# Side transfers on another queue, and decays and scans at other ticks, in a hybrid attention and state-space block

## The chip, the core and the metric

The kernel runs on one core of one Trainium2 chip. The metric is the device time of one execution in microseconds, the median of three runs. A profile of one execution shows each engine's instructions: TensorE (PE, its weight loads PEld), VectorE (DVE), ScalarE (ACT), GpSimd (POOL) and SyncE (SP), which only issues transfers here.

## The reference

One layer and a final norm on x of 256 rows and 2048 columns, in float32:

```
hn = rms_norm(x)
q, k, v, z_a, z_s, xbc, dt, g_a, g_s = split(hn @ w_in)
o_a = sum over three dilated windows of softmax-weighted attention(q, k, v) * silu(z_a)
xs, B, C = split(silu(causal_conv(xbc)))
y = chunked state-space scan of xs * dt with decays exp(cumsum(dt * a)), chunks of 128 rows
y = rms_norm((y + d_skip * xs) * silu(z_s))
merged = sigmoid(g_a) * (o_a @ w_attn) + sigmoid(g_s) * (y @ w_ssm)
out = rms_norm(x + merged @ w_out)
```

Sixteen attention heads of 128 columns; eight groups of the state-space part with eight heads of 64 columns each.

## The kernel before

**Weights and splits.** All weights lie in one array `wall`, cut into units of 128 x 1024 floats (512 KB) in the order in which they are used (`weight_plan`, `FIRST[tag]` is a tag's first unit). `unit(n)` takes a unit from a ring of five slots (`ring`, tag "w", loaded by SP's queue), rounds it to a high part `h` on ScalarE and leaves the rest as a low part `l` on VectorE; h and l have four buffers each. Every product is made of three parts, high by high, high by low and low by high.

**Gemms.** `gemm_a` makes 128 output columns from two units: for each of 16 blocks a matmul of 512 moving columns with h (L329) and one of 256 with l (L332). `gemm_b` makes a gate. `gemm_pair` makes 1024 output columns for v, the attention gate, and the three output projections; it goes over quads (two blocks of rows and two of columns) in an order given by hand (`V_ORDERS` and the like). A quad named in `S_QUADS` takes seven products instead of eight. It needs sums of weight blocks and sums of blocks of the left matrix.

**Side work.** `sum_jobs` makes the sums of weight blocks ahead of time, 37 jobs: `get` loads two pieces, `add` (three units later) subtracts them on VectorE and `spill` writes the sum to DRAM; 18 jobs lie in the groups' loop (place `sums_at`), 19 in the attention (place `th_a`). `keep_left` makes the sums of a left matrix (x, y or o) with `turn_x` and spills them; `fetch_left` reads them back before they are used. All this is hung on units with `behind_unit(n, f)`: f is called once unit n has been converted and gets a piece of h, `behind`. Each transfer is held back by a one-column copy on GpSimd from `behind` into the tile that the transfer then writes (`fetch`, L638, and L247, L251, L432, L903); the transfers themselves are issued by SP, those of `fin` and `fw` by ScalarE.

**Ticks.** Each gemm (each two units of `gemm_b`, each quad of `gemm_pair`) begins with `tick()`; `after(n, f)` calls f n ticks later. In the loop over eight groups (per group one B and one C gemm, four gemms each of xs and zs) the work of a group hangs on the tick of its last xs gemm: `turn` 3 later (L801), four `decays` 2, 3, 4 and 9 later (each loads `acb` by SP and issues six activations, L782 and L786), `scan` 11 later (L820), and then `gather`, which writes yT. Before two of the groups gate gemms add to the lags. After the last group one gate gemm follows, and `tick(final=True)` calls all that is still due.

**Order.** A planner with a simulated timeline orders each engine's instructions within their dependencies, with priorities given in the code; what stands here is the program that it made. `tc.issue_after(ins)` adds an edge: every instruction made in its block on the engine of `ins` stays behind `ins` in that engine's queue.

**Pools.** The left factors of x for v and the attention gate are quads 2, 4, 5, 6 (`SX_X`) and 3 (`SX_V`). Quad 2's has a pool of its own (`xk`), which opens before the pool of the output projection of the state-space part; the others' (`xl`, `vx`) open after it, where that pool was.

Of the kernel before, what the change touches and what calls it, by code (L numbers as in the profile page):

```python
# [15 lines left out]
P = 128  # L16
# [4 lines left out]
GROUPS = 8  # L21
# [14 lines left out]
N_ACT_X = 1  # L36
DT_LAG, CB_LAG, TURN_LAG, GT_LAG, Y_LAG, S_LAG, M_LAG = 2, 5, 3, 2, 11, 2, 2
Y_AFTER = 0, 0
GS_BEFORE = {0: (0, 1), 4: (2,)}
A_ORDERS = {0: (0, 1, 2, 4, 3, 6, 5, 7), 2: (0, 2, 1, 4, 3, 5, 6, 7)}  # L40
V_ORDERS = {0: (0, 2, 4, 1, 3, 5, 6, 7), 2: (0, 2, 1, 4, 3, 5, 6, 7)}
G_ORDERS = {c: (0, 2, 1, 4, 3, 5, 6, 7) for c in (0, 2)}
# [154 lines left out]
def hybrid_block(ctx: ExitStack, tc: tile.TileContext, wall, xt, x, pk_d, cst_d, fw_d, out):  # L197
# [32 lines left out]
    ssm_pool = []  # L230

    def behind_unit(n, f):
        on_unit.setdefault(n, []).append(f)
# [4 lines left out]
    def spill(kept, key, name, src, shape):  # L238
        kept[key] = dram.tile([P, *shape], F32, name=name, tag=name)
        nc.sync.dma_start(kept[key], src)  # L240

    def sum_jobs(jobs, units, places):

        def get(tag, q, t, b11, behind):
            n = FIRST[tag] + 2 * q
            for dst, src in ((t, wall[n + 1]), (b11, wall[n, :, :512])):
                gp.tensor_copy(dst[:, 0:1], behind)  # L247
                nc.sync.dma_start(dst, src)

        def add(tag, q, t, b11, res, behind):  # L250
            gp.tensor_copy(res[:, 0:1], behind)  # L251
            ve.tensor_tensor(res[:, :512], t[:, :512], b11, ALU.subtract)
            ve.tensor_tensor(res[:, 512:], t[:, 512:], res[:, :512], ALU.subtract)
            spill(presum, (tag, q), f"t_{tag[0]}{tag[1]}_{q}", res, [UNIT])

        for n, ((tag, q), u) in enumerate(zip(jobs, units)):
            t, b11, res = places[n % len(places)]
            behind_unit(u, lambda behind, a=(tag, q, t, b11): get(*a, behind))
            behind_unit(u + SUM_LAG, lambda behind, a=(tag, q, t, b11, res): add(*a, behind))

# [6 lines left out]
    def unit(n, shape):  # L267
        if n not in loaded:
            load(n)
        w = loaded.pop(n)  # L270
        h = stream.tile([P, UNIT], F32R, name=f"h{n}", tag="h", bufs=H_BUFS)
        l = stream.tile([P, UNIT], F32R, name=f"l{n}", tag="l", bufs=H_BUFS)
        cuts = (0, UNIT // 2, UNIT) if n < N_FINE else (0, UNIT)
        with tc.high_priority(L_AHEAD) if n >= KT // UB else nullcontext():
            for a, b in zip(cuts, cuts[1:]):
                ac.activation(h[:, a:b], w[:, a:b], AF.Copy)  # L276
                ve.tensor_tensor(l[:, a:b], w[:, a:b], h[:, a:b].bitcast(F32), ALU.subtract)  # L277
        for f in on_unit.pop(n, ()):
            f(h[:, 0:1].bitcast(F32))
        k, m = shape  # L280
        return h.rearrange("p (k m) -> p k m", k=k), l.rearrange("p (k m) -> p k m", k=k)
# [147 lines left out]
    def fetch_left(kept, pool, bufs, key, x, spare, u):  # L429
        def get(behind):  # L430
            sx = new_sx(pool, bufs, spare, f"{key[0]}{key[1]}")
            gp.tensor_copy(sx[:, 0, 0, 0:1], behind)  # L432
            nc.sync.dma_start(sx.bitcast(F32), lefts[key])
            kept[key[1]] = left_parts(sx, x, spare)

        behind_unit(u, get)
# [248 lines left out]
    with tc.tile_pool(name="ssm", bufs=2) as sp:  # L685
# [205 lines left out]
        for c in GS_BEFORE[0]:  # L891
            gates(("gs", c), th_s, yT, hr_x)

        sums_at = big.tile([P, 4, UNIT], F32, name="sums_at", tag="yo1b")
        at = sums_at[:, 3]
        begin = FIRST[("xs", 4)]
        sum_jobs(
            SUMS_SSM, [FIRST[("B", g)] + n for g in range(1, 7) for n in SUM_UNITS],
            [(sums_at[:, 0], sums_at[:, 2, :512], sums_at[:, 1])],
        )  # L900

        def left_x(q, behind):
            gp.tensor_copy(at[:, 0:1], behind)  # L903
            keep_left(("x", q), two_kts(XT, q), 0, at)

# [3 lines left out]
        for g in range(GROUPS):  # L909
# [9 lines left out]
            for t in range(max(4 * g, 1), 4 * g + 4):  # L919
                u, i = divmod(t, 2)  # L920
                acc = project(("xs", t))
                if i == 0:
                    state["xs"].append(new_pair(u, "xs"))
                if t % 4 == 3:
                    gate = 4 * len(GS_BEFORE.get(g + 1, ()))
                    after(TURN_LAG + gate * 3 // 4, lambda a=(g, state): turn(*a))

                    y_lag = Y_LAG + gate
                    for k in range(4):
                        after(GT_LAG + k if k < 3 else y_lag - 2, lambda a=(g, k, cb, state): decays(*a))  # L930
                    after(y_lag, lambda a=(g, state): scan(*a), 1)
# [32 lines left out]

    xk = ctx.enter_context(tc.tile_pool(name="xk", bufs=1))
    sx_of_x = {}

    for n, q in enumerate(SX_X[:1]):
        fetch_left(sx_of_x, xk, 1, ("x", q), two_kts(XT, q), 0, plain_unit(("ssm", 2), 12, Y_ORDERS[2]))
    def room_of(t, n_wt, n_wc):  # L970
# [6 lines left out]
    with tc.tile_pool(name="xp", bufs=1) as xp:  # L977
# [8 lines left out]
        for q in SX_Y:  # L986
            if q in Y_LATE:
                continue
            fetch_left(sxs, xp, sum(s == Y_SPARE[q] for s in Y_SPARE.values()), ("y", q), two_kts(yT, q), Y_SPARE[q], plain_unit(("ssm", 0), Y_ORDERS[0].index(q) - 3 if q in S_QUADS[("ssm", 0)] else 12, Y_ORDERS[0]))
        for c in (0, 2):  # L990
# [22 lines left out]
    dist_c, count_c = dc[:, :384], dc[:, 384:]  # L1013
    behind_unit(FIRST[("v", 2)] + 1, lambda behind: fetch(dc, cst_d[:, :768], behind))
    room = room_of(big.tile([P, 6 * 512], F32, name="room_v", tag="yo0a"), 2, 2)
    with tc.tile_pool(name="vx", bufs=1) as vx:
        tl = big.tile([P, 4, UNIT], F32R, name="tl_v", tag="yo0b")
        room["tl"] = [(tl[:, 2 * n], tl[:, 2 * n + 1]) for n in range(2)]
        for n, q in enumerate(SX_V):
            fetch_left(sx_of_x, vx, len(SX_V), ("x", q), two_kts(XT, q), 0, FIRST[("v", 0)])  # L1020
        for n, q in enumerate(SX_X[1:]):
            fetch_left(sx_of_x, xl, len(SX_X) - 1, ("x", q), two_kts(XT, q), 0, FIRST[("v", 0)] + 1 + n)
        for c in (0, 2):
# [9 lines left out]
    with tc.tile_pool(name="att", bufs=2) as ap:  # L1033
# [33 lines left out]
        def mix(h, pT, za):  # L1067
# [10 lines left out]
            if h % 2 == 1 and q in ATT_QUADS:  # L1078
                keep_left(("o", q), two_kts(oaT, q), 0, mul.tile([P, UNIT], F32, name=f"sxt_o{q}", tag="ht", bufs=2))

        sum_jobs(
            SUMS_ATT, range(FIRST[("q", 0)] + 7, N_UNITS, ATT_EVERY),
            [
                (th_a[:, i, :UNIT], th_a[:, 1, UNIT + 512 * i : UNIT + 512 * i + 512], th_a[:, 0, UNIT:])
                for i in range(2)
            ],
        )
# [16 lines left out]
        for n, q in enumerate(ATT_QUADS):  # L1104
            fetch_left(
                sx_of_o, xl if n else xk, max(1, n and len(SX_X) - 1), ("o", q), two_kts(oaT, q), 0, FIRST[("ga", 2)] + O_BEHIND[n]
            )
# [8 lines left out]
    with tc.tile_pool(name="fin", bufs=2) as fp:  # L1116
# [36 lines left out]
        for n in range(4):  # L1153
            i, cs = n // 2, slice(n % 2 * UNIT, (n % 2 + 1) * UNIT)
            behind_unit(
                FIRST[X_BEHIND[n][0]] + X_BEHIND[n][1],
                lambda behind, i=i, cs=cs: fetch(fin[:, i, cs], x[i * P : (i + 1) * P, cs], behind, nc.scalar),
            )

        fw = big.tile([P, D], F32, name="fw", tag="yo0b")  # L1160
        for n, (tag, u) in enumerate(FW_BEHIND):
            cs = slice(n * UNIT, (n + 1) * UNIT)
            behind_unit(
                FIRST[tag] + u, lambda behind, cs=cs: fetch(fw[:, cs], fw_d[cs].partition_broadcast(P), behind, nc.scalar)
            )
# [106 lines left out]
```

## Time and profile before

| what | us |
|---|---|
| median of three runs (1385.03 to 1385.79) | 1385.75 |
| the profiled execution, first to last instruction | 1383.8 |
| TensorE busy | 1373.6 |
| VectorE busy | 1169.5 |
| ScalarE busy | 835.5 |
| GpSimd busy | 142.0 |

Of the profiled execution the span is known, and its time is taken as the span. It lies 1.95 us below the median of the runs. Busy times overlap, since the engines run side by side; TensorE's granted clock is full up to 1379 us.

### The profile page before, as it was taken

How to read it: one execution, taken by the hardware profiler on the slowest of the kernel's cores; microseconds unless marked ns; L12 is line 12 of the kernel's file. 1: busy time of each engine (PE TensorE's matmuls, PEld its weight loads, DVE VectorE, ACT ScalarE, POOL GpSimd, SP SyncE). 2: the span in 40 equal slices, each digit the busy share in tenths (PEclk: the TensorE clock that was granted, in tenths of full speed). 3: DMA queues.
4: the chain of work that ended last, by engine and by line, in shares of the span. 5: the costliest groups of instructions: out<-in, count | busy, mean ns of one | idle time of the engine just before them, and what ended most of it. 6: DMA issues, size and time to landing. Idle time of an engine off the chain costs nothing.

```text
span 1383.8 us, 20696 instructions
## 1 busy us (share of the span) xinstructions
PE 1373.6 (99%) x7266; PEld 1169.9 (85%) x7266; DVE 1169.5 (85%) x1753; ACT 835.5 (60%) x1306; POOL 142.0 (10%) x226
## 2 busy tenths in 40 slices
PE   9999999999999999999999999999999999999997
PEld 8888888888888888888888888888888888888886
DVE  7898999987799898789889897777877788888897
ACT  7656677675667675766565554544544556655564
POOL 2301111101011100010001001111111000000112
PEclk9999999999999999999999999999999999999999
DMA  9767988868787866668677668888888757865773
GB/s 347 231 187 225 313 254 291 279 224 287 245 266 240 294 212 208 188 224 280 230 259 267 222 209 278 275 275 273 299 288 301 241 161 264 294 222 180 243 273 122
DMA packets 105080, 345.00 MB, mean 249 GB/s; under 512 B 11728, under 2 KB 13712, under 8 KB 104976
## 3 DMA queue, kind: packets, MB, share of 16 engines
q1 hardware_dynamic: 103536, 339.62, 74.0%
q10 hardware_dynamic: 1440, 4.06, 0.8%
q8 instruction: 57, 0.93, 0.3%
q14 instruction: 47, 0.39, 0.1%
HBM read 314.87 MB, written 28.77 MB: 248 GB/s over the span
## 4 chain that ended last, share of the span: by engine, by line
PE 97%; DMA 1%; DVE 1%; ACT 1%; issue 0%; SPq 0%; POOL 0%; POOLq 0%; DVEq 0%; ACTq 0%
PE ps_zs L329 8%; PE ps_xs L329 8%; PE ps_zs L332 4%; PE ps_q L329 4%; PE ps_za L329 4%; PE ps_k L329 4%; PE ps_xs L332 4%; PE ps_ssm L476 3%; PE ps_ssm L477 3%; PE ps_ssm L478 3%; PE ps_q L332 2%; PE ps_k L332 2%; PE ps_za L332 2%; PE ps_gs L414 2%; PE ps_gs L412 2%; PE ps_gs L413 2%
## 5 line engine op out<-in xcount | busy, mean ns | idle before, releaser
L276 ACT ACTIVATE h<-w 128x1024 fp32r<-128x1024 f32 (+1 forms) x398 | 413.9, 1047 | 318.0 <-issue 78.8
L277 DVE TENSOR_TENSOR l<-w,h 128x1024 fp32r<-128x1024 f32 (+1 forms) x398 | 479.4, 1211 | 124.2 <-ACT h L276 121.8
L329 PE MATMUL ps_zs<-XT,h 128*128 128x512 f32 x496 | 176.3, 397 | 0.0
L329 PE MATMUL ps_xs<-XT,h 128*128 128x512 f32 x496 | 175.9, 396 | 0.0
L332 PE MATMUL ps_zs<-XT,l 128*128 128x256 f32 x496 | 139.9, 282 | 0.0
L332 PE MATMUL ps_xs<-XT,l 128*128 128x256 f32 x496 | 139.8, 282 | 0.0
L329 PEld LDWEIGHTS ps_xs<-XT,h 128*128 128x128 f32 x496 | 93.3, 188 | 21.7
L329 PEld LDWEIGHTS ps_zs<-XT,h 128*128 128x128 f32 x496 | 93.4, 188 | 21.2
L332 PEld LDWEIGHTS ps_zs<-XT,l 128*128 128x128 f32 x496 | 93.7, 189 | 1.5 <-issue 0.7
L332 PEld LDWEIGHTS ps_xs<-XT,l 128*128 128x128 f32 x496 | 93.7, 189 | 0.4
L329 PE MATMUL ps_q<-XT,h 128*128 128x512 f32 x256 | 92.5, 405 | 0.2 <-ACT h L276 0.2
L329 PE MATMUL ps_k<-XT,h 128*128 128x512 f32 x256 | 89.9, 395 | 0.0
L329 PE MATMUL ps_za<-XT,h 128*128 128x512 f32 x256 | 89.7, 394 | 0.0
L543 ACT ACTIVATE ha<-wa 128x1024 fp32r<-128x1024 f32 x43 | 45.4, 1055 | 46.4 <-DMA wa<-in_wall 10.9
L332 PE MATMUL ps_q<-XT,l 128*128 128x256 f32 x256 | 71.2, 278 | 0.0
L332 PE MATMUL ps_k<-XT,l 128*128 128x256 f32 x256 | 71.1, 278 | 0.0
L332 PE MATMUL ps_za<-XT,l 128*128 128x256 f32 x256 | 71.1, 278 | 0.0
L544 DVE TENSOR_TENSOR la<-wa,ha 128x1024 fp32r<-128x1024 f32 x43 | 52.5, 1220 | 11.9 <-ACT ha L543 11.8
L782 ACT ACTIVATE gt<-acb,acT 128x128 f32<-128x128 f32 x128 | 44.2, 391 | 23.7 <-DMA acb<-acum_d 21.9
L329 PEld LDWEIGHTS ps_q<-XT,h 128*128 128x128 f32 x256 | 48.2, 188 | 11.5 <-ACT h L276 0.6
L329 PEld LDWEIGHTS ps_za<-XT,h 128*128 128x128 f32 x256 | 48.1, 188 | 11.3
L329 PEld LDWEIGHTS ps_k<-XT,h 128*128 128x128 f32 x256 | 48.1, 188 | 11.2
(688 smaller groups left out, 3325.1 us busy)
## 6 DMA issues: line engine op xcount, KB each, us to landing
w<-in_wall SPq DMA_DIRECT2D x394, 512.0 KB, 4.7
wa<-in_wall SPq DMA_DIRECT2D x43, 512.0 KB, 4.9
th_a<-in_wall SPq DMA_DIRECT2D x19, 512.0 KB, 5.6
sums_at<-in_wall SPq DMA_DIRECT2D x18, 512.0 KB, 4.7
acb<-acum_d SPq DMA_DIRECT2D x32, 256.0 KB, 4.0
t_ssm<-sums_at SPq DMA_DIRECT2D x13, 512.0 KB, 4.1
wt<-t_ssm SPq DMA_DIRECT2D x13, 512.0 KB, 5.4
th_a<-in_wall SPq DMA_DIRECT2D x19, 256.0 KB, 6.0
```

The costliest lines, as they stand in the source:

```text
L276: ac.activation(h[:, a:b], w[:, a:b], AF.Copy)
L277: ve.tensor_tensor(l[:, a:b], w[:, a:b], h[:, a:b].bitcast(F32), ALU.subtract)
L329: pe.matmul(acc, h[:, kk, :], m, start=(kt == 0), stop=False)
L332: pe.matmul(acc[:, S:], l[:, kk, :], m[:, :S], start=False, stop=(kt == KT - 1))
L412: pe.matmul(accs[i], xh, h[:, kk], start=(kt == 0), stop=False)
L413: pe.matmul(accs[i], xh, l[:, kk], start=False, stop=False)
L476: pe.matmul(acc, xh, h, start=start, stop=False)
L477: pe.matmul(acc, xh, l, start=False, stop=False)
L478: pe.matmul(acc, xl, h, start=False, stop=stop)
L543: ac.activation(h, src, AF.Copy)
L544: ve.tensor_tensor(l, src, h.bitcast(F32), ALU.subtract)
L782: ac.activation(g4[:, n, b], acb[:, j, b // 2 * P : b // 2 * P + P], AF.Relu, scale=-1.0, bias=sc[:, h : h + 1],)
```

## The change

- `side` issues a transfer from ScalarE's queue, behind the last converted unit's `h` (`here["high"]`), with no copy on GpSimd. It is used for the loads of `sum_jobs`, for `fetch_left`, for `dc`, `fin` and `fw`. `spill` issues on GpSimd's queue instead of SP's.
- `sum_jobs` subtracts in place (no third tile), behind the last `l`; the groups' loop has two places instead of one. `left_x` has no copy either.
- The four decays of a group come 2, 4, 6 and 9 ticks after its last xs gemm instead of 2, 3, 4 and 9; in group 6 they come 2, 3, 4 and 5 later and its scan 7 later, in group 7 they begin before its last xs gemm and its scan comes 4 later (all scans were 11 later).
- `V_ORDERS[0]` begins 0, 1, 2, 4 instead of 0, 2, 4, 1.
- The pool `xk` goes: all four left factors of x share `xl` and are fetched by v's first units; that of `SX_V` is fetched three units later than before. The left factors of o use the same four places.
- The last left factor of o is made in a slot of the weight ring instead of a tile of `mul`.

```diff
...
 N_ACT_X = 1
-DT_LAG, CB_LAG, TURN_LAG, GT_LAG, Y_LAG, S_LAG, M_LAG = 2, 5, 3, 2, 11, 2, 2
+DT_LAG, CB_LAG, TURN_LAG, Y_LAG, S_LAG, M_LAG = 2, 5, 3, 11, 2, 2
+GT_LAGS, END_LAGS, END_LAG = (2, 4, 6, 9), (2, 3, 4, 5), (7, 4)
 Y_AFTER = 0, 0
...
 A_ORDERS = {0: (0, 1, 2, 4, 3, 6, 5, 7), 2: (0, 2, 1, 4, 3, 5, 6, 7)}
-V_ORDERS = {0: (0, 2, 4, 1, 3, 5, 6, 7), 2: (0, 2, 1, 4, 3, 5, 6, 7)}
+V_ORDERS = {0: (0, 1, 2, 4, 3, 5, 6, 7), 2: (0, 2, 1, 4, 3, 5, 6, 7)}
 G_ORDERS = {c: (0, 2, 1, 4, 3, 5, 6, 7) for c in (0, 2)}
...
 
+    here = {}
+
+    def side(dst, src, queue=nc.scalar):
+        with tc.issue_after(here["high"]):
+            queue.dma_start(dst, src)
+
     def behind_unit(n, f):
...
         kept[key] = dram.tile([P, *shape], F32, name=name, tag=name)
-        nc.sync.dma_start(kept[key], src)
+        gp.dma_start(kept[key], src)
 
...
 
-        def get(tag, q, t, b11, behind):
+        def get(tag, q, t, b11):
             n = FIRST[tag] + 2 * q
-            for dst, src in ((t, wall[n + 1]), (b11, wall[n, :, :512])):
-                gp.tensor_copy(dst[:, 0:1], behind)
-                nc.sync.dma_start(dst, src)
-
-        def add(tag, q, t, b11, res, behind):
-            gp.tensor_copy(res[:, 0:1], behind)
-            ve.tensor_tensor(res[:, :512], t[:, :512], b11, ALU.subtract)
-            ve.tensor_tensor(res[:, 512:], t[:, 512:], res[:, :512], ALU.subtract)
-            spill(presum, (tag, q), f"t_{tag[0]}{tag[1]}_{q}", res, [UNIT])
+            side(t, wall[n + 1])
+            side(b11, wall[n, :, :512])
+
+        def add(tag, q, t, b11):
+            with tc.issue_after(here["low"]):
+                ve.tensor_tensor(t[:, :512], t[:, :512], b11, ALU.subtract)
+                ve.tensor_tensor(t[:, 512:], t[:, 512:], t[:, :512], ALU.subtract)
+            spill(presum, (tag, q), f"t_{tag[0]}{tag[1]}_{q}", t, [UNIT])
 
         for n, ((tag, q), u) in enumerate(zip(jobs, units)):
-            t, b11, res = places[n % len(places)]
-            behind_unit(u, lambda behind, a=(tag, q, t, b11): get(*a, behind))
-            behind_unit(u + SUM_LAG, lambda behind, a=(tag, q, t, b11, res): add(*a, behind))
+            a = tag, q, *places[n % len(places)]
+            behind_unit(u, lambda behind, a=a: get(*a))
+            behind_unit(u + SUM_LAG, lambda behind, a=a: add(*a))
 
...
             for a, b in zip(cuts, cuts[1:]):
-                ac.activation(h[:, a:b], w[:, a:b], AF.Copy)
-                ve.tensor_tensor(l[:, a:b], w[:, a:b], h[:, a:b].bitcast(F32), ALU.subtract)
+                here["high"] = ac.activation(h[:, a:b], w[:, a:b], AF.Copy).ins
+                here["low"] = ve.tensor_tensor(l[:, a:b], w[:, a:b], h[:, a:b].bitcast(F32), ALU.subtract).ins
         for f in on_unit.pop(n, ()):
...
             sx = new_sx(pool, bufs, spare, f"{key[0]}{key[1]}")
-            gp.tensor_copy(sx[:, 0, 0, 0:1], behind)
-            nc.sync.dma_start(sx.bitcast(F32), lefts[key])
+            side(sx.bitcast(F32), lefts[key])
             kept[key[1]] = left_parts(sx, x, spare)
...
         sums_at = big.tile([P, 4, UNIT], F32, name="sums_at", tag="yo1b")
-        at = sums_at[:, 3]
+        at = sums_at[:, 2]
         begin = FIRST[("xs", 4)]
...
             SUMS_SSM, [FIRST[("B", g)] + n for g in range(1, 7) for n in SUM_UNITS],
-            [(sums_at[:, 0], sums_at[:, 2, :512], sums_at[:, 1])],
+            [(sums_at[:, n], sums_at[:, 3, n * 512 : n * 512 + 512]) for n in range(2)],
         )
...
         def left_x(q, behind):
-            gp.tensor_copy(at[:, 0:1], behind)
-            keep_left(("x", q), two_kts(XT, q), 0, at)
+            with tc.issue_after(here["low"]):
+                keep_left(("x", q), two_kts(XT, q), 0, at)
 
...
                     state["xs"].append(new_pair(u, "xs"))
+                if t == 4 * GROUPS - 2:
+                    for k in range(4):
+                        after(1 + k, lambda a=(g, k, cb, state): decays(*a))
                 if t % 4 == 3:
...
 
-                    y_lag = Y_LAG + gate
-                    for k in range(4):
-                        after(GT_LAG + k if k < 3 else y_lag - 2, lambda a=(g, k, cb, state): decays(*a))
+                    y_lag = ((Y_LAG,) * (GROUPS - 2) + END_LAG)[g] + gate
+                    for k, lag in enumerate(END_LAGS if g == GROUPS - 2 else GT_LAGS):
+                        if g < GROUPS - 1:
+                            after(lag + gate // 2, lambda a=(g, k, cb, state): decays(*a))
                     after(y_lag, lambda a=(g, state): scan(*a), 1)
...
 
-    xk = ctx.enter_context(tc.tile_pool(name="xk", bufs=1))
     sx_of_x = {}
 
-    for n, q in enumerate(SX_X[:1]):
-        fetch_left(sx_of_x, xk, 1, ("x", q), two_kts(XT, q), 0, plain_unit(("ssm", 2), 12, Y_ORDERS[2]))
     def room_of(t, n_wt, n_wc):
...
                 continue
-            fetch_left(sxs, xp, sum(s == Y_SPARE[q] for s in Y_SPARE.values()), ("y", q), two_kts(yT, q), Y_SPARE[q], plain_unit(("ssm", 0), Y_ORDERS[0].index(q) - 3 if q in S_QUADS[("ssm", 0)] else 12, Y_ORDERS[0]))
+            fetch_left(sxs, xp, sum(s == Y_SPARE[q] for s in Y_SPARE.values()), ("y", q), two_kts(yT, q), Y_SPARE[q], plain_unit(("ssm", 0), max(Y_ORDERS[0].index(q) - 3, 0) if q in S_QUADS[("ssm", 0)] else 12, Y_ORDERS[0]))
         for c in (0, 2):
...
     dist_c, count_c = dc[:, :384], dc[:, 384:]
-    behind_unit(FIRST[("v", 2)] + 1, lambda behind: fetch(dc, cst_d[:, :768], behind))
+    behind_unit(FIRST[("v", 2)] + 1, lambda behind: side(dc, cst_d[:, :768]))
     room = room_of(big.tile([P, 6 * 512], F32, name="room_v", tag="yo0a"), 2, 2)
...
         for n, q in enumerate(SX_V):
-            fetch_left(sx_of_x, vx, len(SX_V), ("x", q), two_kts(XT, q), 0, FIRST[("v", 0)])
-        for n, q in enumerate(SX_X[1:]):
-            fetch_left(sx_of_x, xl, len(SX_X) - 1, ("x", q), two_kts(XT, q), 0, FIRST[("v", 0)] + 1 + n)
+            fetch_left(sx_of_x, vx, len(SX_V), ("x", q), two_kts(XT, q), 0, FIRST[("v", 0)] + 3)
+        for n, q in enumerate(SX_X):
+            fetch_left(sx_of_x, xl, len(SX_X), ("x", q), two_kts(XT, q), 0, FIRST[("v", 0)] + n)
         for c in (0, 2):
...
             if h % 2 == 1 and q in ATT_QUADS:
-                keep_left(("o", q), two_kts(oaT, q), 0, mul.tile([P, UNIT], F32, name=f"sxt_o{q}", tag="ht", bufs=2))
+                last = q == ATT_QUADS[-1]
+                place = ring(f"sxt_o{q}") if last else mul.tile([P, UNIT], F32, name=f"sxt_o{q}", tag="ht", bufs=2)
+                keep_left(("o", q), two_kts(oaT, q), 0, place)
 
...
             SUMS_ATT, range(FIRST[("q", 0)] + 7, N_UNITS, ATT_EVERY),
-            [
-                (th_a[:, i, :UNIT], th_a[:, 1, UNIT + 512 * i : UNIT + 512 * i + 512], th_a[:, 0, UNIT:])
-                for i in range(2)
-            ],
+            [(th_a[:, i, :UNIT], th_a[:, i, UNIT : UNIT + 512]) for i in range(2)],
         )
...
             fetch_left(
-                sx_of_o, xl if n else xk, max(1, n and len(SX_X) - 1), ("o", q), two_kts(oaT, q), 0, FIRST[("ga", 2)] + O_BEHIND[n]
+                sx_of_o, xl, len(SX_X), ("o", q), two_kts(oaT, q), 0, FIRST[("ga", 2)] + O_BEHIND[n]
             )
...
                 FIRST[X_BEHIND[n][0]] + X_BEHIND[n][1],
-                lambda behind, i=i, cs=cs: fetch(fin[:, i, cs], x[i * P : (i + 1) * P, cs], behind, nc.scalar),
+                lambda behind, i=i, cs=cs: side(fin[:, i, cs], x[i * P : (i + 1) * P, cs]),
             )
...
             behind_unit(
-                FIRST[tag] + u, lambda behind, cs=cs: fetch(fw[:, cs], fw_d[cs].partition_broadcast(P), behind, nc.scalar)
+                FIRST[tag] + u, lambda behind, cs=cs: side(fw[:, cs], fw_d[cs].partition_broadcast(P))
             )
...
         spare = big.tile([P, 8, 512], F32, name="spare", tag="yo0a")
```

## Rows read from the trace of the kernel before

**Rows 1.** The page's first part: span; busy us (share) x instructions.

```profile
span 1383.8 us, 20696 instructions
...
PE 1373.6 (99%) x7266; PEld 1169.9 (85%) x7266; DVE 1169.5 (85%) x1753; ACT 835.5 (60%) x1306; POOL 142.0 (10%) x226
```

**Rows 2.** Stretches: length, then PE, PEld, DVE, ACT, POOL busy, in us.

```profile
76.80:558.00 481.20, 481.20 (x2847) 415.66 (x2846) 425.57 (x702) 324.33 (x609) 49.11 (x103) 1.00 0.78 253
...
558.00:583.50 25.50, 25.50 (x138) 20.72 (x136) 19.01 (x21) 19.02 (x36) 0.00 (x0) 1.00 0.66 200
...
583.50:828.00 244.50, 244.29 (x1084) 201.99 (x1081) 216.33 (x238) 143.26 (x162) 10.35 (x13) 1.00 0.71 239
...
746.00:756.00 10.00, 10.00 (x45) 8.28 (x45) 9.89 (x14) 4.23 (x5) 0.00 (x0) 1.00 0.66 211
```

**Rows 3.** TensorE's list of waits: us in total, times, longest.

```profile
PE warm L623 <- DVE ssq L620: 1.4, 1, 1.4
PE ps_first L377 <- ACT h L276: 0.3, 1, 0.3
PE ps_q L329 <- ACT h L276: 0.2, 1, 0.2
```

**Rows 4.** Timeline of TensorE: its last matmul (start us, us).

```profile
1375.22 0.28 PE L478 MATMUL ps_right<-h,mT 128*128 128x256 f32 x1
```

**Rows 5.** Timeline of TensorE: first matmuls of four gemms.

```profile
135.55 0.39 PE L329 MATMUL ps_xs<-XT,h 128*128 128x512 f32 x1
...
141.10 0.39 PE L329 MATMUL ps_zs<-XT,h 128*128 128x512 f32 x1
...
158.59 0.40 PE L329 MATMUL ps_xs<-XT,h 128*128 128x512 f32 x1
...
164.24 0.40 PE L329 MATMUL ps_zs<-XT,h 128*128 128x512 f32 x1
```

**Rows 6.** Groups in 135.6:141.1, 158.6:164.2, 76.8:558: busy us, mean ns | idle.

```profile
L329 PE MATMUL ps_xs<-XT,h 128*128 128x512 f32 x16 | 5.6, 391 | 0.0
...
L329 PE MATMUL ps_xs<-XT,h 128*128 128x512 f32 x16 | 5.7, 399 | 0.0
...
L329 PE MATMUL ps_zs<-XT,h 128*128 128x512 f32 x496 | 176.3, 397 | 0.0
```

**Rows 7.** Groups of instructions of GpSimd: the costliest.

```profile
L251 POOL COPY th_a<-h 128x1 f32<-128x1 f32 x19 | 23.6, 1241 | 157.8 <-ACT h L276 157.8
```

**Rows 8.** Timeline of ScalarE: a transfer issued by its queue.

```profile
1296.34 0.34 ACTq L639 DMA_DIRECT2D fin<-in_x  x1
```

**Rows 9.** Stretch from 130 to 160 us, columns as in rows 2.

```profile
130.00:160.00 30.00, 30.00 (x174) 26.33 (x173) 28.63 (x48) 22.02 (x41) 4.89 (x10) 1.00 0.87 291
```

**Rows 10.** Timeline around the first fetch of a left factor of y.

```profile
580.83 2.82 PE L820 MATMUL yp<-gt,xdt 128*64 128x256 f32 x32
...
586.68 1.06 ACT L276 ACTIVATE h<-w 128x1024 fp32r<-128x1024 f32 x1
...
593.94 0.43 POOL L432 CAST sx_y<-h 128x1 fp32r<-128x1 f32 x1 [63.29 <-DVE sxt_y L450]
```

**Rows 11.** DMA issues by line: count, KB each, median us to landing.

```profile
t_ga<-th_a SPq DMA_DIRECT2D x8, 512.0 KB, 5.4
```

**Rows 12.** Timeline of GpSimd in the attention.

```profile
863.05 1.24 POOL L251 COPY th_a<-h 128x1 f32<-128x1 f32 x1 [8.74 <-ACT h L276]
...
878.04 1.24 POOL L247 COPY th_a<-h 128x1 f32<-128x1 f32 x1 [1.62 <-ACT h L276]
```

**Rows 13.** ScalarE's list of waits: us in total, times, longest.

```profile
ACT gt L782 <- DMA acb<-acum_d: 21.9, 18, 2.6
```

**Rows 14.** Timeline of TensorE within an xs gemm.

```profile
247.90 0.40 PE L329 MATMUL ps_xs<-XT,h 128*128 128x512 f32 x1
248.13 0.39 PE L329 MATMUL ps_zs<-XT,h 128*128 128x512 f32 x1
```

**Rows 15.** Timeline of TensorE: first matmul of v.

```profile
748.54 0.39 PE L476 MATMUL ps_v<-h,XT 128*128 128x512 f32 x1
```

## Prediction

> **What bounds the kernel now.** I read the engines' totals first. TensorE is busy for 1373.6 us of a span of 1383.8 us, VectorE for 1169.5, ScalarE for 835.5, GpSimd for 142.0 [rows 1]. A share that high can hide waits, so the stages come next: the group loop, the last gate gemm and the two product stages after it keep TensorE busy for all their time but 0.2 us, while VectorE has 6 to 56 us to spare in each [rows 2]. The list of TensorE's own waits agrees: three in the whole program, 1.9 us together, two of them at the start (the warm-up waits for a memset, the first product for its first weights) and one of 0.2 us at the border from v to q [rows 3]. The last matmul begins at 1375.2 and lasts 0.28 us [rows 4]; the 8.3 us after it are the last row's norm and the output's transfer, and the diff leaves their instructions alone. So what bounds the kernel is TensorE's own list of instructions, and an edit gains only if it shortens that list's run; taking work off a queue or an engine that TensorE does not wait for is worth nothing.
>
> One thing in TensorE's time can still move. The projections run as pairs, a 512-column matmul with the high part and a 256-column one with the low part. From the first matmul of one xs gemm to the first of the next, some take 141.10 - 135.55 = 5.55 us (call them brisk) and some 164.24 - 158.59 = 5.65 us (broad) [rows 5], with the same instructions, no wait and the same granted clock. The 512-column matmul reads 391 ns in the brisk gemm, 399 ns in the broad one and 397 ns over all of zs [rows 6], so some (397 - 391) / (399 - 391) = 75% of the 76 gemms of xs, zs, B and C (31 + 31 + 7 + 7 by the plan) are broad. All broad gemms turned brisk would give 0.75 x 76 x 0.10 = 5.7 us, all brisk gemms turned broad would take 1.9 us. What other matmuls stand in between seems to choose; I come back to it.
>
> **The change, part by part.** *Copies on GpSimd.* Each side transfer was held back by a one-column copy on GpSimd: three for each of 37 sum jobs, five for the left factors of x, 15 for fetches of left factors, seven for dc, fin and fw, 138 in all. They go. Their means run up to 1241 ns [rows 7], about the length of the VectorE instruction that starts beside them, so at most 138 x 1.24 = 171 us by that row, and no more than GpSimd's 142.0 in fact. No engine that TensorE waits for stands behind them: 0 us.
>
> *Loads and fetches to ScalarE's queue.* 37 x 2 loads, 15 fetches and dc are 90 issues that leave SP's queue. One issue on ScalarE took 0.34 us [rows 8]; with the 0.1 us of gap beside it, 90 x 0.45 = 41 us more for an engine with 835.5 of 1383.8 us. In the tightest stretch, 130 to 160 us, ScalarE has 22.0 of 30 us [rows 9] and gets two jobs, 1.8 us. Cover: 8 us of idle ScalarE there. Cost 0; with that cover gone, 0.45 us an issue would reach TensorE.
>
> *The wait that comes with them.* Behind an issue in ScalarE's queue stand the conversions that TensorE needs next; formerly a late place held up GpSimd's copy and SP's loads. The nearest row that shows such a wait is GpSimd's first fetch of a left factor of y, which starts at 593.94 after 63.3 us, while the conversions of those units began at 586.68 [rows 10]: the room belongs to tiles that the last scan's results pass through, and that scan runs from 580.83 [rows 10]. In ScalarE's queue this would be 593.94 - 586.68 - 1.06 = 6.2 us of hold. The change draws the scan forward: lag 4 after the last xs gemm falls two ticks ahead of the end of the last gs gemm, and a tick is about one gemm [rows 5], so its gather ends some 11 us earlier, before that conversion. The hold goes where it was about to come from: 0. Bounds: 0, and 6.2 us less the lead of up to three units that four h buffers allow (3 x 5.55 / 2 = 8.3), also 0. The gather takes 6 us of VectorE into a stretch where it has 19.0 of 25.5 [rows 2], and the last multiplication of the decays leaves it: it fits.
>
> *Spills on GpSimd's queue.* 52 writes of sums and left factors leave SP's queue. No row shows a transfer issued by GpSimd. Below it costs what SP's did, 5.4 us to landing [rows 11]; above, I take the room before anyone needs the place: in the attention a job's sum starts at 863.05 and the same place is loaded again at 878.04 [rows 12], 15.0 us, less 1.4 us for the sum itself, so 13.6 us. Between 5.4 and 13.6 us nothing waits, and I take 0, since the nearest row is 8 us away from that edge. (A rule speaks against this part. The Trainium skill, page "SBUF — State Buffer", section "SBUF: two separate sides", says that GpSimd itself writes the descriptors of a transfer that it issues, and cannot while VectorE holds the port pair that they share in a two-port instruction; its example grows from 0.62 to 3.1 us. By the row the sum is 1385.2. By the rule a spill would land some 2.5 us later, an estimate from that example, and the sum would be the same; only a lock-out of over 8 us would turn it into the held queue below. No run here shows it yet.)
>
> *Decays over nine gemms.* A group's four steps had lags 2, 3, 4 and 9 and get 2, 4, 6 and 9; the same 192 activations and 32 loads. ScalarE waited 21.9 us in 18 pieces for those loads [rows 13]; some of it goes. TensorE waited for none of it: 0. A trace of the bunching is left in TensorE's order, though: at 248.13 one matmul of zs stands within an xs gemm [rows 14], which the planner did because it took the weights to be late there; gemms before it are brisk, those after it are broad. That is in group 3's gemms; groups 5 to 7 have such a place each. Some 2.5 gemms follow each until the next matmul of another kind: 4 x 2.5 x 0.10 = 1.0 us if all four vanish, 0 if none does. I take half, -0.5 us.
>
> *Order of v, and no pool of its own for a left factor of x.* The first product quad comes third instead of second, and its factor is fetched later, behind the conversion of v's first unit. TensorE starts on that unit at 748.54 us [rows 15], so it is converted before; a fetch then lands by 754 at the latest [rows 11], and two plain quads are 48 matmuls ahead of its use. Where v starts VectorE is busy for 9.89 of 10 us [rows 2], and a plain quad gives it two long instructions instead of five; TensorE did not wait there before, so 0. Five product quads then follow in a row, where three did; up to their end both orders hold the same work, so the later point is no worse.
>
> *A weight slot for the last left factor of o, no copy before fin and fw, sums in place.* One of five weight slots is taken for one turn and one spill; the four others and four h buffers hide it: 0.
>
> **Sum.** 1383.8 - 0.5 = 1383.3 us of span. The runs' median, 1385.75, stands 1.95 us above the profiled span; with that added, **1385.2 us**.
>
> **Rivals.** *TensorE falls into the brisk pace (faster).* Spreading the decays changes the planner's picture in the whole group loop, and more than the four places flip. From half of the 5.7 us it counts as a gain: 1380.1 to 1382.9. For it: the pace did change at 248 without a wait. Against: after a scan and after most B-C products it is broad again, and those keep their places in six of eight groups. The other way round it takes at most 1.9 us, 1387.7, still no difference.
>
> *ScalarE's queue is held (slower).* Place: the 19 jobs of the attention, each with two loads that wait for the spill of two jobs earlier; point: a spill that lands later than 13.6 us stops the conversions, and beyond some 6 us more TensorE stops. Price: 17 jobs by what is over; 0.2 us over is 3.4 us, 1389, half a microsecond over 1394. Against: 5.4 us landing before. For it: no row shows such a transfer, and 17 of them stand in line. (The Trainium skill's rule above would work through this place.)
>
> *The change does not do what it says.* Order is written by the planner, and with slack everywhere it may put the issues where they were: 1385.75.
>
> **Chances.** Forecast 0.62 (its own range, from all pace terms, 1383.0 to 1387.7); no effect on the order 0.06; brisk pace 0.16; held queue 0.16. Within 0.2% of 1385.75, that is 2.8 us, about what a measurement can tell from no change, 0.68; faster 0.16; slower 0.16. The range 1381.5 to 1390 leaves out less than half of the brisk case and half of the held one.
>
> **What would show it.** Right: TensorE's busy time 1373 us and its list of waits still under 2.5 us; GpSimd's one-column copies gone; 0.34 us issues on ScalarE with no pause of conversions behind them; no matmul of zs within xs. Wrong: TensorE waiting for h in the attention or at 584 us (held queue), gemms of 5.55 us throughout the group loop (brisk pace), or a tail that is not 8.3 us.

## The result: 0.4% slower, nearly all of it at one border

The changed kernel takes 1391.26 us (median of five runs, 1389.03 to 1391.71) where the kernel before takes 1385.52 (five runs): a ratio of 1.0038, 95% interval 1.0025 to 1.005. By the bound that the prediction set (0.2%) that is slower; the forecast was 1385.2 us, and its range ended at 1390.

The profiled execution took 1391.55 us; its span of 1389.8 is 6.0 us more than before. Its page, first part and DMA queues:

```profile
span 1389.8 us, 20434 instructions
...
PE 1374.6 (99%) x7266; PEld 1169.5 (84%) x7266; DVE 1166.6 (84%) x1753; ACT 838.3 (60%) x1306; POOL 69.3 (5%) x140
...
q1 hardware_dynamic: 82448, 276.30, 59.7%
q10 hardware_dynamic: 14400, 40.77, 8.8%
q0 software_dynamic: 7328, 26.61, 5.0%
```

By the sizes of the transfers, q10 is ScalarE's queue (4.06 MB before) and q0 GpSimd's (nothing before): they moved as the change says. Beside [rows 1] TensorE has the same 7266 matmuls and only 1.0 us more of busy time, and GpSimd lost half its work: the copies are gone. So most of the 6.0 us must lie in pauses and ends. TensorE's list of waits has one that was not there [rows 3]:

```profile
PE ptp L1070 <- DVE p L1065: 3.0, 1, 3.0
PE ps_first L383 <- ACT h L282: 1.6, 1, 1.6
PE warm L628 <- DVE ssq L625: 1.4, 1, 1.4
PE ps_q L335 <- ACT h L282: 0.2, 1, 0.2
```

The transposes of a head's probabilities wait 3.0 us for the softmax. The timeline of TensorE shows which head, and what follows:

```profile
1123.27 0.40 PE L483 MATMUL pp_ga<-htt,sx_x 128*128 128x512 f32 x1
1126.64 0.30 PE L1070 MATMUL ptp<-cst,p 128*128 128x128 f32 x1 [2.97 <-DVE p L1065]
1126.69 1.17 PE L481 MATMUL ps_ga<-h,XT 128*128 128x512 f32 x4
1127.70 0.38 PE L1070 MATMUL ptp<-cst,p 128*128 128x128 f32 x2
1127.94 0.66 PE L482 MATMUL ps_ga<-l,XT 128*128 128x512 f32 x1
1128.40 0.63 PE L483 MATMUL ps_ga<-h,XT 128*128 128x512 f32 x1
1128.82 0.63 PE L482 MATMUL ps_ga<-l,XT 128*128 128x512 f32 x1
```

It is head 15, at the border from the attention's projections to ga. In the kernel before, matmuls of ga fill the time up to the same transposes:

```profile
1121.34 0.58 PE L476 MATMUL ps_ga<-h,XT 128*128 128x512 f32 x1
...
1129.74 0.28 PE L1064 MATMUL ptp<-cst,p 128*128 128x128 f32 x1
```

In the changed kernel, after the pause the matmuls start 0.43 us apart, where the same ones start 0.23 us apart elsewhere. The table of stretches says why (columns as in rows 2; the seventh number is the granted clock):

```profile
1121.00:1124.00 3.00, 2.54 (x14) 1.61 (x12) 2.85 (x9) 1.34 (x4) 0.00 (x0) 1.00 0.00 0
1124.00:1126.60 2.60, 0.00 (x0) 0.00 (x0) 2.56 (x14) 2.34 (x5) 0.00 (x0) 1.00 0.00 0
...
1128.00:1131.40 3.40, 3.40 (x10) 2.62 (x10) 3.40 (x5) 1.55 (x3) 0.53 (x1) 0.52 0.74 224
```

TensorE stood still, and behind that the granted clock was 0.52, the lower of its two levels (1.2 GHz), for 3.4 us.

The next table is worked out from the starts of first matmuls in the timelines of both kernels, and from the ends. It places the 6.0 us:

| stretch | before, us | after, us | difference |
|---|---|---|---|
| start to the first matmul of dt | 29.08 | 29.52 | +0.44 |
| from there to the first of v | 719.47 | 719.00 | -0.47 |
| to the first of q | 76.36 | 76.59 | +0.23 |
| to the first of head 15's za | 289.44 | 289.48 | +0.04 |
| to the first of the attention's gemm (the border and ga) | 90.57 | 95.79 | **+5.22** |
| to the end of the last matmul | 170.59 | 170.58 | -0.01 |
| behind it | 8.26 | 8.83 | +0.57 |

The first and third lines differ by as much from trace to trace (28.83 to 29.98 and 76.11 to 77.34 over those of this study). The second does not, and will be taken apart below.

What was TensorE out of work for? ScalarE's timeline of the kernel before converts the first two weight units of ga at 1111.70 and 1114.48:

```profile
1111.70 1.06 ACT L276 ACTIVATE h<-w 128x1024 fp32r<-128x1024 f32 x1 [1.44 <-issue]
1114.48 1.06 ACT L276 ACTIVATE h<-w 128x1024 fp32r<-128x1024 f32 x1 [1.71 <-PE ps_k L329]
```

ScalarE's timeline of the changed kernel:

```profile
1110.13 0.37 ACT L389 ACTIVATE lo_q<-ps_q 128x256 f32<-128x256 f32 x1
1114.84 0.39 ACT L389 ACTIVATE lo_k<-ps_k 128x256 f32<-128x256 f32 x1 [4.34 <-PE ps_k L338]
1120.33 0.38 ACT L389 ACTIVATE lo_za<-ps_za 128x256 f32<-128x256 f32 x1 [5.10 <-PE ps_za L338]
...
1124.44 0.80 ACT L1057 ACTIVATE p<-t,st 128x128 f32<-128x128 f32 x2 [0.26 <-DVE st L1055]
1125.15 1.04 ACT L282 ACTIVATE h<-w 128x1024 fp32r<-128x1024 f32 x1
...
1126.66 1.04 ACT L282 ACTIVATE h<-w 128x1024 fp32r<-128x1024 f32 x1
```

The two `h` at 1125.15 and 1126.66 are those units. ScalarE idles 4.3 and 5.1 us ahead of lo_k and lo_za, but the order written for it has these conversions behind head 15's `p`. Their weights were there: in SyncE's order ga's two units are the last of the six `w` loads that went out by 1104.6, and the next `w` waits until 1127.91 for the slot of the first of them.

```profile
1086.00 18.64 SPq L271 DMA_DIRECT2D w<-in_wall  x6
...
1127.91 2.06 SPq L271 DMA_DIRECT2D w<-in_wall  x2
```

So an order, not a transfer, left TensorE without matmuls while head 15's softmax ran on the other engines.

### The profile page after: what moved, and what is told of

It is laid out like the page before. It is cut to its first block, busy times and chain, and to the rows that moved or that the text cites. A ratio compares the mean times of both kernels' runs of the same rounds, so it can differ in the third digit from the quotient of the medians.

```text
span 1389.8 us, 20434 instructions
## 1 busy us (share of the span) xinstructions
PE 1374.6 (99%) x7266; PEld 1169.5 (84%) x7266; DVE 1166.6 (84%) x1753; ACT 838.3 (60%) x1306; POOL 69.3 (5%) x140
## 4 chain that ended last, share of the span: by engine, by line
PE 93%; DVE 3%; DMA 1%; issue 1%; ACT 1%; SPq 0%; POOL 0%; POOLq 0%; DVEq 0%; ACTq 0%
PE ps_zs L335 8%; PE ps_xs L335 8%; PE ps_zs L338 4%; PE ps_q L335 4%; PE ps_za L335 4%; PE ps_k L335 4%; PE ps_xs L338 4%; PE ps_ssm L481 3%; PE ps_ssm L482 3%; PE ps_ssm L483 3%; PE ps_q L338 2%; PE ps_k L338 2%; PE ps_za L338 2%; PE ps_gs L418 2%; PE ps_gs L419 2%; PE ps_gs L420 2%
```

## Experiments

Theory A: the edit of the last left factor of o, to which the prediction gave 0. `mix(13)` asks for a slot of the weight ring just ahead of ga's first units in the program. Rivals: the spills on GpSimd's queue, or the side loads on ScalarE's.

**1. The slot undone.**

```diff
-                place = ring(f"sxt_o{q}") if last else mul.tile(...)
+                place = mul.tile(...)
```

> The changed kernel with one line undone: the sums of the last left factor of o stand in a buffer of the attention's own pool again, not in a slot of the weight ring. Theory A (the slot, asked for in the program ahead of the first two weight units of ga, puts their conversions behind head 15's softmax, so TensorE stands still for 3.0 us at 1123.7 and then runs 3.4 us at half clock): 1385.0 to 1386.3, no wait of TensorE before head 15's transposes, units 0 and 1 of ga converted near 1112 and 1115 again. Theory B (the spills on GpSimd's queue, or side loads issued by ScalarE, hold something at the border of ga): nothing of them is changed here, 1390.5 to 1392.

1388.68 us; 1.0022 times before, 1.0013 to 1.003. Both missed. The wait for head 15 is gone, but another has come:

```profile
PE ps_first L383 <- ACT h L282: 1.6, 2, 1.3
PE pp_ga L481 <- ACT htu L548: 1.5, 1, 1.5
PE warm L628 <- DVE ssq L625: 1.4, 1, 1.4
PE pp_ga L482 <- DVE ltu L549: 0.5, 1, 0.5
```

The chain that ended last leads from there to the spill of these same sums:

```profile
1131.07 6.99 DMA sxd_o<-sxt_o
...
1138.13 1.06 ACT htu L548
...
1139.22 1.24 DVE ltu L549
...
1140.50 0.50 PE pp_ga L482
```

In its own buffer the last left factor is followed by a converted product weight of ga (`htu`), which must wait until the spill has landed; on GpSimd's queue that took 7.0 us. In the kernel before, where the same spill went by SyncE, ScalarE already waited 2.94 us for it, and TensorE did not:

```profile
1135.09 1.06 ACT L543 ACTIVATE htu<-wa 128x1024 fp32r<-128x1024 f32 x1 [2.94 <-DMA sxd_o<-sxt_o]
```

The stretch from za to the attention's gemm is 93.24 us, 2.67 more than before. Theory B had the right part, GpSimd's queue, but in a place that the changed kernel no longer has.

**2. The slot alone, on the kernel before.** The same one line the other way round.

> The kernel before with that one line alone: the last left factor of o takes a slot of the weight ring, everything else as before. Theory A: 1389.5 to 1391.5, with a wait of about 3 us before head 15's transposes and matmuls of ga at 427 in place of 227 ns behind it. Theory B: 1385.0 to 1386.

1390.81 us; 1.0037, 1.0025 to 1.005. As theory A says. The wait is the same one, and za to attn takes 95.65 us:

```profile
PE ptp L1064 <- DVE p L1059: 3.0, 1, 3.0
```

**3. The slot asked for later.** The turn and its slot come two ticks later in the program.

```diff
+                if last:
+                    after(2, lambda q=q: keep_left(("o", q), two_kts(oaT, q), 0, ring(f"sxt_o{q}")))
```

> The changed kernel, slot kept, but the slot is asked for, and the left factor turned, two steps later in the program, behind the units of the first two quads of ga. If the place in the program's order is the cause (A1): 1385.0 to 1386.3, as with a buffer of its own. If the missing slot itself is (A2: four slots are too few while it is held): the wait stays or moves to the next units, 1388 to 1392.

1385.72 us; 1.0001, 0.9992 to 1.001: A1. za to attn is 90.58 us, and ScalarE's order has the two units where they belong, ahead of lo_k:

```profile
1111.19 1.06 ACT L282 ACTIVATE h<-w 128x1024 fp32r<-128x1024 f32 x1 [1.44 <-issue]
1113.96 1.06 ACT L282 ACTIVATE h<-w 128x1024 fp32r<-128x1024 f32 x1 [1.71 <-PE ps_k L335]
1114.93 0.37 ACT L389 ACTIVATE lo_k<-ps_k 128x256 f32<-128x256 f32 x1
```

The slot, held later, still leaves four for the weights; that costs nothing. What cost was the place at which it was asked for. The turn moved too, but in experiment 1 it stood at its old place without that wait.

**4. The pause filled.** 24 transposes of the identity, of no use to the result, into the bank that head 15's transposes then overwrite.

```diff
+            for i in range(24 if h == 15 else 0):
+                pe.transpose(tps[:, :P], ident, ident)
```

> The changed kernel with 24 transposes of the identity, of no use to the result, ahead of head 15's own transposes in the same bank, about 2.6 us of work by the pace of the transposes in the trace (0.11 us each), so TensorE is busy in most of the pause. If the half pace behind the pause is the granted clock's answer to the pause (A): the 427 ns steps go, 1389.0 to 1389.9, near the one run of the changed kernel at 1389.03 whose mean clock was 0.999. If it has another cause (the operands' arrival, a queue): 1390.8 to 1391.8.

1389.33 us; 1.0029, 1.0019 to 1.0039: 1.9 us below the changed kernel with more work. Timeline of TensorE:

```profile
1121.95 2.78 PE L1070 MATMUL ptp<-cst 128*128 128x128 f32 x24
...
1125.69 0.33 PE L1072 MATMUL ptp<-cst,p 128*128 128x128 f32 x1 [0.26 <-DVE p L1065]
...
1127.90 0.40 PE L483 MATMUL ps_ga<-h,XT 128*128 128x512 f32 x1
1128.13 0.40 PE L482 MATMUL ps_ga<-l,XT 128*128 128x512 f32 x1
```

The steps are 0.23 us again, and the granted clock is 1.00 from 1121 to 1133:

```profile
1121.00:1133.00 12.00, 11.62 (x65) 9.60 (x65) 11.83 (x28) 8.36 (x14) 0.53 (x1) 1.00 0.39 125
```

za to attn takes 94.23 us, so of the 5.22 us the clock took 95.79 - 94.23 = 1.56 and the missing work 3.66. The one run of the changed kernel at 1389.03 fits: its mean clock was 0.999, that of the others 0.996 or 0.997.

**5. One spill back to SyncE.** Experiment 1 with the last of the 52 spills issued by SyncE.

> The kernel with the sums in their own buffer (1388.7), and of its 52 spills the last one, of the last left factor of o, issued by SyncE again. Theory C (that buffer is next taken by a converted weight of ga, and the spill of it lands 7.0 us after its issue on GpSimd's queue where SyncE's took 4.3 us, so ScalarE converts 3 us late and TensorE waits 2.1 us): 1385.0 to 1386.2, no wait of TensorE in ga. Rival (the buffer's order, or ScalarE's side issues, make that conversion late whatever queue spills): 1388 to 1389.

1385.78 us; 1.0, 0.9991 to 1.0009: theory C. The spill landed in 4.3 us, and TensorE has no wait in ga.

**6. That spill alone, on the kernel before.**

```diff
-        nc.sync.dma_start(kept[key], src)
+        queue = gp if key == ("o", ATT_QUADS[-1]) else nc.sync
+        queue.dma_start(kept[key], src)
```

> The kernel before with one of its 52 spills, that of the last left factor of o, issued by GpSimd and nothing else changed. If the landing on GpSimd's queue is late by itself (C): as in the kernel with the sums in their own buffer, TensorE waits some 2 us for the converted weight htu in ga, 1387.5 to 1388.9. If it needs ScalarE's side loads or the other GpSimd spills beside it: 1385.3 to 1386.2.

1388.61 us; 1.0023, 1.0013 to 1.0034: theory C again. It landed in 7.0 us and the waits are those of experiment 1. Five of its eight runs took 1387.1 to 1388.7 at mean clocks of 0.998 or 0.999, three 1390.7 to 1391.4 at 0.996 or 0.997; the profiled one is of these, and the stretch behind its pause shows the lower clock:

```profile
1139.00:1142.40 3.40, 1.40 (x5) 0.59 (x4) 1.66 (x2) 2.75 (x3) 0.00 (x0) 0.98 0.16 63
1142.40:1145.70 3.30, 3.30 (x9) 2.63 (x8) 3.30 (x4) 2.69 (x4) 0.00 (x0) 0.50 0.66 202
```

**7 to 9. The other parts, undone one by one in the kernel of experiment 3.** All 52 spills to SyncE; decays and scans at the old lags; side transfers to SyncE (`queue=nc.sync` in `side`).

> The kernel with the slot asked for later (1385.7), with all 52 spills issued by SyncE again. If GpSimd's queue costs only where a buffer waits for a landing, the time in the gemms stays; its ends may differ: the last 8.9 us behind the last matmul (8.3 us before) go back to 8.3 if GpSimd's queue lengthens them. With it 1384.9 to 1385.6, without 1385.4 to 1386.2; a spill that holds SyncE's weight loads up would show as 1386.5 or more.

> The kernel with the slot asked for later (1385.7), with decays and scans of all groups at the lags of the kernel before. If the 0.29 us by which the stretch from dt to the last gemm of zs runs shorter in the changed kernel and in its variants, and the 0.48 us up to the end of ssm, come from the decays and scans: both go, and the time is 1385.9 to 1386.4. If they come from the copies or the side loads: both stay, 1385.3 to 1386.0.

> The kernel with the slot asked for later (1385.7), with the side transfers of ScalarE's queue issued by SyncE, among its weight loads. If the 90 issues on ScalarE cost nothing, as the prediction has it, and SyncE has room for them too: 1385.3 to 1386.2. If ScalarE's issues held conversions up unseen: up to 1 us faster, 1384.5 to 1385.2. If SyncE's order holds weight loads behind side loads that wait for their buffer: 1387 or more.

The three took 1385.5 us (1.0, 0.9991 to 1.0008), 1385.32 (0.9997, 0.9988 to 1.0005) and 1389.5 (1.0031, 1.002 to 1.0043). In time the first two can't be told from before. The starts of matmuls tell more, since with one order of TensorE they repeat to 0.01 us (the changed kernel and experiments 1, 3, 4 and 5 all have 523.16 in the second column):

| kernel | dt to group 7's C | dt to the last gemm of zs | dt to v | behind the last matmul |
|---|---|---|---|---|
| before | 474.00 | 523.45 | 719.47 | 8.26 |
| slot later (3) | 473.13 | 523.16 | 719.00 | 8.92 |
| and spills on SyncE (7) | 473.36 | 523.39 | 719.22 | 8.26 |
| and old decays and scans (8) | 473.08 | 522.52 | 718.54 | 8.96 |
| and side transfers on SyncE (9) | 475.48 | 525.51 | 721.86 | 8.26 |

- Up to group 7's C the old lags and the new ones give the same time to 0.05 us: the decays at 2, 4, 6 and 9 are worth nothing. From C to the last zs the new lags take 523.16 - 473.13 = 50.03 us and the old ones 49.44: the new lags of the last two groups, decays and scans together, cost 0.6 up to there. At v 0.4 of it is left (719.00 - 718.54 = 0.46, of which 0.05 stands ahead of C).
- GpSimd's spills are worth 0.23 us up to C. Copies gone, sums in place and side loads on ScalarE, all that is left, make 0.64 of the 0.87 us. None of this is a wait removed: between dt and v TensorE waits for nothing in the kernel before [rows 3], in the changed kernel or in experiment 10. What differs is the order of its matmuls. Up to v it differs in two of 3926 places between experiments 3 and 7, a transpose and a matmul of C that change places, and in 270 between before and experiment 10. So the gains come with TensorE's pace in another order, as with the prediction's brisk and broad gemms, and not from a freed queue; what makes one order faster stays open.
- On SyncE the side transfers take 2.9 us more up to v. So of the two queues ScalarE's is the better place for them here; TensorE's list of waits shows one of 1.5 us in that stretch that the kernel of experiment 3 does not have:

```profile
PE ps_xs L338 <- DVE l L283: 1.5, 1, 1.5
```

Of experiment 8's two cases the second came, and more: the gain up to v is not from the decays and scans, which cost some of it. Experiment 7 came out by its first case, with the end at 8.26 us again (by the median alone its first two cases overlap); experiment 9 by the time of its third.

**10. Old lags and SyncE's spills together.**

> The kernel with the slot asked for later (1385.7), with decays and scans at the lags of the kernel before and all 52 spills issued by SyncE: of the change, the side transfers by ScalarE, the missing copies, the sums in place, the order of v, the pool and the slot are left. If the stages add up (dt to v 718.5 us with the old lags, 0.2 more for SyncE's spills; 90.6 from the last za to attn; 8.26 behind the last matmul instead of 8.9): TensorE ends near 1374.8, span 1382.8 to 1383.4, 1384.6 to 1385.3. If the gains of the two parts are of the same choice of gemm paces and don't add: 1385.3 to 1386.0.

1386.28 us; 1.0004, 0.9996 to 1.0013: above both cases. The stretch from dt to v does add up (718.82 by the traces), but v to q took 76.92 in the profiled execution, and the median is no better than before. Why the median lies 0.9 us above the profiled execution (1385.35) no trace shows. No version here beats the kernel before by what can be measured; experiments 3, 5, 7 and 8 match it.

## Why the prediction was wrong

- **Bound.** Right: TensorE's list sets the time, and the loss is a hole in it. None of the rivals goes through that hole: the slow one was a held queue of ScalarE, which did not come.
- **"One of five weight slots is taken for one turn and one spill; the four others and four h buffers hide it: 0."** This is the step that failed, by 5.22 us. It asked whether four slots are enough, and they are (experiment 3). It did not ask what stands behind the request for the slot in the program: ga's first two units, which were TensorE's cover for head 15's softmax. Without them 3.66 us are lost and, behind the pause, 1.56 to the lower clock (experiments 2 to 4). That the planner writes the order so because slots are given out in the program's order, and units behind an unfilled slot count as late, is argued from the orders of experiments 2 and 3; the planner's simulated times were not looked at, so this reason is not shown.
- **Spills on GpSimd's queue: 0.** Right for the changed kernel, by luck. The room of 13.6 us was read from the sum jobs of the attention, where it holds (below). The buffer of the last left factor has hardly any, as ScalarE's wait of 2.94 us for it in the kernel before shows: its spill in 7.0 us instead of 4.3 costs 2.67 us (experiments 1, 5, 6). The slot is what takes that wait away, so the two edits belong together, and the prediction, which took them apart, saw neither price. The landings by line (count, KB, median us) in the changed kernel:

```profile
t_ssm<-sums_at POOLq DMA_DIRECT2D x13, 512.0 KB, 4.1
t_ga<-th_a POOLq DMA_DIRECT2D x8, 512.0 KB, 7.3
t_attn<-th_a POOLq DMA_DIRECT2D x7, 512.0 KB, 7.6
```

  Two of them with all spills on SyncE (experiment 7):

```profile
t_ga<-th_a SPq DMA_DIRECT2D x8, 512.0 KB, 6.9
...
t_attn<-th_a SPq DMA_DIRECT2D x7, 512.0 KB, 7.2
```

  In the kernel before t_ga took 5.4 us [rows 11]. Most of its rise is there with SyncE's queue too (6.9), so it came with other parts of the change; GpSimd's queue adds 0.4 us to these two lines. The last left factor alone shows the queue itself: 7.0 against 4.3 us with nothing else changed (experiment 6). In experiment 1 the queue's first packet moved 1.5 us after that issue and the last 5.2 us after the first; of an earlier left factor (issued at 985.3) all packets moved within some 1.6 us.

  The Trainium skill, page "SBUF — State Buffer", section "SBUF: two separate sides", which the prediction weighed, gave some 2.5 us more, an estimate from its example; the 2.7 us of the last left factor agree in size, the 0.4 of t_ga do not. Whether the shared port is the cause no run here shows. The prediction's inference that 2.5 us would change nothing was wrong for that one spill.
- **Copies, 138 x up to 1.24 us: 0; side loads on ScalarE: 0.** No wait went with them, as predicted, but with the sums in place they gave about 0.6 us through the order of TensorE's matmuls (experiments 7 and 10). ScalarE held up no conversion that TensorE waited for: the stages of v and the attention are as long as before. The rival of a held queue did not come; the longest median, 7.6 us, is far from 13.6. A pair of issues takes 0.82 us, near the 0.9 that was costed.

```profile
865.01 0.82 ACTq L237 DMA_DIRECT2D th_a<-in_wall  x2
```

- **Decays: -0.5.** Wrong in mechanism. The matmul of zs within an xs gemm [rows 14] is still there:

```profile
248.51 0.39 PE L335 MATMUL ps_zs<-XT,h 128*128 128x512 f32 x1
```

  The spread decays gave 0; the new lags of the last two groups took 0.6 up to the last zs and 0.4 up to v, which the sum did not have. ScalarE's waits for the decays' loads went from 21.9 us [rows 13] only to 21.0. That the net gain up to v, 0.47 us, is near the predicted 0.5 is luck: the prediction put down to the decays what the copies, the sums in place and the side loads gave.
- **Wait at ssm's start, with the scan drawn forward: 0.** TensorE does not wait there. With the old scan lags (experiment 8) it did not either, so the reason given, the earlier scan, was not needed: there ScalarE converted three weight units before it issued that fetch at 592.78. The lead was also misread: the gather's last step ended at 587.65 instead of 593.72, some 6 us earlier and not 11.
- **Pace.** Up to v 0.47 us was gained; the rival of several microseconds did not come. The prediction's guess that the matmuls in between choose the pace fits the one changed place of experiment 7; what makes a gemm brisk or broad was not tested.
- **Tail, 8.3 us.** 8.83, and 8.3 again in experiments 7 and 9. It is 8.7 to 9.0 us in the kernels where both GpSimd's queue and ScalarE's carry these transfers; the reason was not looked for.

## What to carry to other kernels

A buffer from a ring costs more than its capacity: look at what stands behind the request in the program, and whether that work is the cover of a chain elsewhere (here a softmax that only two weight units hid). When a transfer changes its queue, follow each buffer to its next user, the odd one of 52 as well as the many. Edits that look separate can hide one another: the spill's new queue costs 3 us alone and nothing beside the slot, and undoing the slot, which costs 5 us alone, won back only half of it because it laid the spill bare (experiments 1, 2, 3 and 6). So the undoing of one edit is no proof of what it costs.

## What was not expected of the hardware

- A pause of 3.0 us cost another 1.56 us through the clock, at 0.52 for 3.4 us, in most runs but not in all. Two pauses of 2.0 us together did so in three of eight runs of experiment 6 and, by its mean clock of 0.997, in one of eleven of experiment 1. Work of no use in the pause made the kernel 1.9 us faster.
- With the same order of TensorE's instructions a stretch of 523 us repeats to 0.01 us between the profiled executions of different kernels, while one transpose and one matmul that change places make 0.23 us (experiment 7). So starts of matmuls settle differences of 0.2 us that medians of eleven runs can't.
